# Gates of an RG-LRU group on 64-row halves put together by DMA, skipped zero products, time-step sums on four column groups, and down-weight sums moved to the FFN

## The chip, the cores and the metric

The kernel runs on one core of a Trainium2 chip. The metric is the device time of one execution in microseconds (us), the median over runs. A core has a matrix engine (TensorE), two engines for element-wise work (VectorE, ScalarE), GpSimd, and SyncE (SP), which here only issues DMAs; ScalarE issues DMAs too. Matrix results land in PSUM, everything else lives in SBUF (128 partitions) or in DRAM.

## The reference

One decoder layer on 2048 rows of 1024 numbers, all in float32. The normalised input goes through one projection. Its first 2048 columns feed an RG-LRU group, the rest a Mamba-2 SSD group; both outputs are normalised, joined, and projected back; a SwiGLU FFN of width 2816 follows. The parts that the change touches:

```
# RG-LRU: 16 blocks of 64 channels, each with its own 64x64 gate weights
r = sigmoid(einsum("btki,kij->btkj", xb, w_a) + b_a)
i = sigmoid(einsum("btki,kij->btkj", xb, w_x) + b_x)
log_a = -8 * r * softplus(-lam);  a = exp(log_a)
u = sqrt(-expm1(2 * log_a)) * (i * xf)
h_t = a_t * h_(t-1) + u_t

# SSD, in chunks of 128 time steps, 16 heads of 64, state of 128
a_cs = cumsum(dt * A) within a chunk
y_diag = (C B^T * exp(segsum(a))) x          # inside a chunk
states = carried from chunk to chunk (zero before the first)
y_off = exp(a_cs) * C * (state before the chunk)

# FFN
f = (silu(h @ w_gate) * (h @ w_up)) @ w_down
```

## The kernel before

**Precision.** A product of float32 quality is made of three matrix instructions on the type fp32r, high half times high, high times low, low times high (`mm3`, lines 135 to 137; `split`, lines 130 and 131, makes the halves: a cast on ScalarE, a subtraction on VectorE). Smaller products of plain float32 are listed as two instructions each.

**First stage (lines 260 to 720).** The 2048 time steps are two blocks (`b`) of 1024. Per block the kernel walks over the 37 column tiles of the input projection. Weights of a tile are loaded by SP (line 218) into one of the four `raw` buffers and split. For each tile, `col_product` issues 48 instructions of 128 columns by 512 into a `pp` buffer of PSUM (two of these). The mixes of a tile are Python generators (`ssd_mix`, `lru_mix`) whose pieces are woven into the column products of the next tile by `site` (`SITES` sets how many), so the small products stand between long runs of column products; a scheduler then settles the order on each engine. The small products use the two `pq` buffers of PSUM.

**The gates (`gates`, 363 to 379; `lru_mix`, 381 to 418).** For each of eight tiles of 128 channels, two 64-channel blocks stand side by side, so the weights of one gate are put as two 64x64 blocks on the diagonal of a 128x128 matrix, with zeros elsewhere. `lru_mix` splits the convolved input `lx` into `lh` and `ll` (lines 384, 385) and issues 12 instructions of 128 rows by 512: two gates, two halves of the time, three of `mm3`. ScalarE then runs two Tanh (393), Exp, Tanh, Square, and a square root (397 to 403), VectorE the rest up to the scan over time. Two different function tables are needed, so two table loads stand in it.

**The SSD group.** `ssd_dt3` (446 on) sums the time steps with a triangular matrix: eight products of 16 columns (line 456), one copy of 16x1024 (459), and one DMA to DRAM (`cs_dr`), which every mix reads back spread over partitions (520, 530). `ssd_mix` makes the states of the chunks (`pst`, 544; the carry `U`, 547), their part in the output (`po`, 551), and the part inside a chunk (`py`, 560), whose products are 64 columns wide and alternate between the two halves of the columns.

**Down-weight sums (`wdn_sums`, 569 to 580).** The FFN multiplies 2x2 blocks with seven products instead of eight, so sums of weight blocks are needed. For each of 11 `k`, four blocks of the down weights are loaded, combined by four subtractions (line 575 is the first) and stored to `t_dr`; table `WS` (line 31) puts these into the gate stage.

**FFN.** For each of 22 column tiles `fi` of a block, gate and up weights are loaded (740, 741) into two `raw` buffers, split and summed (744 on), and multiplied: seven products of 12 instructions each.

Of the kernel before, what the change touches and what calls it, by code (L numbers as in the profile page):

```python
# [15 lines left out]
P = 128  # L16
# [3 lines left out]
TB = 1024  # L20
# [10 lines left out]
WS = ((0, 2, 2, 0, 0, 0, 0, 0), (0, 2, 2, 1, 1, 1, 0, 0))  # L31
# [15 lines left out]
def hybrid_layer(ctx: ExitStack, tc: tile.TileContext, x, xT, w_in, w_dt, pack, heads, rows, wa, wx, w_out, w_gu, w_dn, out):  # L47
# [220 lines left out]
    with ExitStack() as fr:  # L268
# [95 lines left out]
        def gates(b, bd):  # L364
            st = wide("L").rearrange("p j (t k) l -> p (j t) k l", k=2)
            v.memset(st, 0.0)
            for j, ww in enumerate((wa, wx)):
                for h in range(2):
                    a.dma_start(out=st[64 * h:64 * h + 64, :, j, 64 * h:64 * h + 64],
                                in_=ww.rearrange("(t two) i j -> two i t j", two=2)[h])  # L370
            if b == 0:
                a.copy(out=bd, in_=st)
            res = []
            for q, z in enumerate(("Bt", "SM")):
                lo = tp.tile([P, 4, 2, P], F32R, name=z, bufs=1)
                qs = slice(4 * q, 4 * q + 4)
                v.tensor_sub(out=lo, in0=st[:, qs], in1=bd[:, qs].bitcast(F32))
                res.append(lo)
            return res

        def lru_mix(b, i, lx, gl, acc, bdl):
            th = []
# [12 lines left out]
            ci = c2[:, i:i + 1]  # L395
            av = t4()
# [4 lines left out]
            v.scalar_tensor_tensor(out=a2, in0=a2, scalar=1.0, in1=th[0], op0=ALU.add, op1=ALU.mult)  # L401
# [45 lines left out]
        def ssd_dt3(b, dt, dta):  # L447
# [7 lines left out]
            for c in range(NC):  # L455
                te.matmul(pr[0:NH, c * P:(c + 1) * P], lhsT=dta[:, c, :], rhs=tri, start=True, stop=True)
# [711 lines left out]
```

## Time and profile before

| | |
|---|---|
| median of 3 runs | 2625.59 us (2624.54 to 2626.57) |
| the profiled execution | 2623.91 us |
| its span, first to last instruction | 2622.1 us |
| TensorE busy | 2608.5 us, 99% of the span, 12357 matrix instructions |
| VectorE, ScalarE busy | 1849.3 us (71%), 1127.7 us (43%) |
| granted TensorE clock | 1.0 throughout |
| chain that ended last | TensorE 94%, VectorE 3%, ScalarE 1%, DMA 1% |

The profiled execution took 1.8 us more than its span and lies 1.7 us under the median. Matrix instructions are pipelined and overlap, so the time listed for one is longer than the step from its start to the next one's start; the price of one is read from starts.

### The profile page before, as it was taken

What the parts mean: (1) busy time and instruction counts of PE and PEld (TensorE: products, weight loads), DVE (VectorE), ACT (ScalarE), POOL (GpSimd) and SP (SyncE); (2) the same over time, 40 slices, a digit from 0 to 9 for tenths busy, and PEclk for the clock granted to TensorE, in tenths of its full rate; (3) what the DMA queues carried; (4) which work ended last, traced back from release to release, by engine and by line L of the source; (5) the groups of instructions that cost most, each with busy time, mean ns of one, the idle gap of its engine ahead of it and who ended that gap; (6) DMA issues with size and microseconds to landing.
All of it is one profiled execution on the core that took longest, in us unless ns stands there. A gap on an engine that the chain in (4) does not pass through costs nothing.

```text
span 2622.1 us, 31852 instructions
## 1 busy us (share of the span) xinstructions
PE 2608.5 (99%) x12357; PEld 2169.2 (83%) x12357; DVE 1849.3 (71%) x2698; ACT 1127.7 (43%) x1357; POOL 1.1 (0%) x8
## 2 busy tenths in 40 slices
PE   9999999999999999999999999999999999999998
PEld 8888888788888888888888888888888888888887
DVE  7997888878777867544478776778667774334676
ACT  7543466754544776333254332233222222322443
POOL 0000000000000000000000000000000000000000
PEclk9999999999999999999999999999999999999999
DMA  5332462224234526543464332235323234444664
GB/s 212 112 130 74 130 211 78 73 82 136 74 109 154 195 96 209 166 132 122 137 207 143 115 120 101 93 136 173 117 86 120 96 100 168 152 141 150 212 246 141
DMA packets 190279, 357.27 MB, mean 136 GB/s; under 512 B 18568, under 2 KB 91664, under 8 KB 190128
## 3 DMA queue, kind: packets, MB, share of 16 engines
q1 hardware_dynamic: 89504, 257.09, 30.4%
q10 hardware_dynamic: 100624, 98.15, 10.8%
q8 instruction: 97, 1.59, 0.2%
q14 instruction: 54, 0.44, 0.1%
HBM read 254.38 MB, written 100.80 MB: 135 GB/s over the span
## 4 chain that ended last, share of the span: by engine, by line
PE 94%; DVE 3%; ACT 1%; DMA 1%; issue 1%; SPq 0%; DVEq 0%; ACTq 0%
PE pf L136 16%; PE pf L135 16%; PE pf L137 16%; PE pp L135 11%; PE pp L137 11%; PE pp L136 11%; PE pq L136 3%; PE pq L137 3%; PE pq L135 3%; PE pq L560 1%; PE pq L539 1%; PE pq L551 1%; DMA L<-cs_dr 1%; DVE lx L309 1%; PE pq L523 1%
## 5 line engine op out<-in xcount | busy, mean ns | idle before, releaser
L135 PE MATMUL pp<-hx,s_hi 128*128 128x512 f32 x1392 | 547.2, 393 | 0.5 <-ACT s_hi L130 0.5
L137 PE MATMUL pp<-hx,s_lo 128*128 128x512 f32 x1392 | 543.8, 391 | 0.5 <-DVE s_lo L131 0.5
L136 PE MATMUL pp<-hx,s_hi 128*128 128x512 f32 x1392 | 543.1, 390 | 0.6 <-DVE hx L251 0.6
L130 ACT CAST s_hi<-raw 128x1024 fp32r<-128x1024 f32 (+1 forms) x167 | 170.3, 1022 | 373.6 <-PE pp L136 100.2
L135 PEld LDWEIGHTS pp<-hx,s_hi 128*128 128x128 f32 x1392 | 261.4, 188 | 56.1 <-issue 1.9
L137 PEld LDWEIGHTS pp<-hx,s_lo 128*128 128x128 f32 x1392 | 261.4, 188 | 55.5 <-DVE s_lo L131 0.8
L136 PEld LDWEIGHTS pp<-hx,s_hi 128*128 128x128 f32 x1392 | 261.5, 188 | 53.8 <-DVE hx L251 1.0
L135 PE MATMUL pf<-hx,s_hi 128*128 128x512 f32 x704 | 274.0, 389 | 0.0
L136 PE MATMUL pf<-hx,s_hi 128*128 128x512 f32 x704 | 273.9, 389 | 0.0
L137 PE MATMUL pf<-hx,s_lo 128*128 128x512 f32 x704 | 273.9, 389 | 0.0
L1008 DVE TENSOR_TENSOR d_lo<-draw,d_hi 128x1024 fp32r<-128x1024 f32 (+1 forms) x110 | 121.2, 1129 | 172.0 <-ACT d_hi L1007 171.8
L131 DVE TENSOR_TENSOR s_lo<-raw,s_hi 128x1024 fp32r<-128x1024 f32 (+1 forms) x167 | 197.9, 1187 | 61.4 <-ACT s_hi L130 57.1
L130 ACT CAST s_hi<-S 128x1024 fp32r<-128x1024 f32 x86 | 90.3, 1050 | 254.8 <-PE pf L136 239.1
L1007 ACT CAST d_hi<-draw 128x1024 fp32r<-128x1024 f32 (+1 forms) x110 | 104.7, 980 | 214.1 <-PE pf L136 181.1
L136 PE MATMUL pf<-d_lo,d_hi 128*128 128x512 f32 x504 | 196.1, 389 | 0.0
L137 PE MATMUL pf<-d_hi,d_lo 128*128 128x512 f32 x504 | 195.9, 389 | 0.0
L135 PE MATMUL pf<-d_hi 128*128 128x512 f32 x504 | 194.6, 389 | 0.0
L137 PEld LDWEIGHTS pf<-hx,s_lo 128*128 128x128 f32 x704 | 132.1, 188 | 27.4
L135 PEld LDWEIGHTS pf<-hx,s_hi 128*128 128x128 f32 x704 | 132.1, 188 | 27.4
L136 PEld LDWEIGHTS pf<-hx,s_hi 128*128 128x128 f32 x704 | 132.1, 188 | 27.4
L309 DVE SCALAR_TENSOR_TENSOR lx<-xr,pk,lx 128x1024 f32<-128x1024 f32 x108 | 138.2, 1280 | 10.2 <-ACT lx L306 9.1
L137 PE MATMUL pf<-hy,s_lo 128*128 128x512 f32 x356 | 138.5, 389 | 0.0
(342 smaller groups left out, 4512.8 us busy)
## 6 DMA issues: line engine op xcount, KB each, us to landing
raw<-w_gu_dram SPq DMA_DIRECT2D x86, 512.0 KB, 4.3
f_dr<-fo ACTq DMA_DIRECT2D x154, 256.0 KB, 4.5
raw<-w_in_dram SPq DMA_DIRECT2D x72, 512.0 KB, 3.4
draw<-f_dr SPq DMA_DIRECT2D x57, 512.0 KB, 4.4
L<-cs_dr SPq DMA_DIRECT2D x32, 512.0 KB, 5.5
g_dr<-t ACTq DMA_DIRECT2D x32, 512.0 KB, 3.3
raw<-g_dr SPq DMA_DIRECT2D x32, 512.0 KB, 4.9
raw<-h_dr SPq DMA_DIRECT2D x26, 512.0 KB, 4.2
```

The lines of the kernel that those rows point to most:

```text
L130: a.copy(out=hi, in_=raw)
L131: v.tensor_sub(out=lo, in0=raw, in1=hi.bitcast(F32))
L135: te.matmul(o, lhsT=wh, rhs=hi, start=start, stop=False)
L136: te.matmul(o, lhsT=wh, rhs=lo, start=False, stop=False)
L137: te.matmul(o, lhsT=wl, rhs=hi, start=False, stop=stop)
L309: v.scalar_tensor_tensor(out=y, in0=xr[:, k:k + TB], scalar=cw(k), in1=y, op0=ALU.mult, op1=ALU.add)
L523: te.transpose(pt[:, c].rearrange("p j d -> p (j d)"), xc[:, c * P:(c + 1) * P], ident)
L539: te.matmul(pst[:, c, :], lhsT=Bt[:, c, :], rhs=xe[:, c].rearrange("p j d -> p (j d)"), start=True, stop=True)
L551: te.matmul(po[:, c, :], lhsT=(sc[:, xi, :] if c == 0 else U[:, c - 1, :]), rhs=C[:, c * P:(c + 1) * P], start=True, stop=True)
L560: te.matmul(py[64 * j:64 * j + 64, c, :], lhsT=xd[:, c, j, :], rhs=L[:, j, c, :], start=True, stop=True)
L1007: a.copy(out=hi, in_=r)
L1008: v.tensor_sub(out=lo, in0=r, in1=hi.bitcast(F32))
```

## The change

- **Gates.** The weights of a tile are no longer put on a diagonal: rows 0 to 63 hold the blocks of r and i of the first 64 channels side by side, rows 64 to 127 those of the second 64 (i and r). Each of the 12 instructions of a mix now reads 64 rows, and its two halves `h` alternate between rows 0 to 63 and 64 to 127, into two `pq` buffers. The result of each half holds r and i of 64 channels on different partitions; after Tanh, four DMAs on SP of 64 partitions by 1024 (line 394 of the new kernel) put r together in one tile and i in another. The last mix of the last block does without them: four Tanh of 64 partitions each write to the right place.
- **Chain after the gates.** The Square and one Tanh of the full rate go; Tanh of half the rate takes its place, and (1 + a) is multiplied in later on VectorE, so its number of instructions there stays.
- **Weights of the gates** are arranged once, not once per block.
- **Skipped.** The product of the first chunk of the first block with a state that is zero (line 551, `c = 0`), and the last chunk's state of the last block, which nobody reads (line 544, with its two VectorE operations), for each of 8 mixes.
- **Time-step sums.** The eight products go to four groups of 32 columns; four copies of 16x256 on ScalarE and VectorE by turns and four DMAs take the place of one copy and one DMA.
- **Down-weight sums** go to the gate tiles 8 to 18 of the FFN's first block, and use two `raw` buffers each instead of two tiles of the first stage.

```diff
-        def gates(b, bd):
-            st = wide("L").rearrange("p j (t k) l -> p (j t) k l", k=2)
-            v.memset(st, 0.0)
...
+        def gates(hi, lo):
+            st = wide("L")[:, 0]
+            for h in range(2):
+                for j, ww in enumerate((wa, wx)):
+                    q = slice(64 * (h ^ j), 64 * (h ^ j) + 64)
+                    a.dma_start(out=st[64 * h:64 * h + 64, :, q],
                                 in_=ww.rearrange("(t two) i j -> two i t j", two=2)[h])
...
-            for j in range(2):
-                pr = pq.tile([P, TB], F32, name="pq")
-                for hh in range(2):
-                    s = slice(hh * HB, (hh + 1) * HB)
-                    mm3(pr[:, s], bd[:, i, j, :], bdl[i // 4][:, i % 4, j, :], lh[:, s], ll[:, s], True, True)
-                t = t4()
-                a.activation(out=t, in_=pr, func=AF.Tanh, scale=0.5, bias=hb[:, 8 * j + i:8 * j + i + 1])
-                th.append(t)
+            prs = [pq.tile([P, TB], F32, name="pq") for _ in range(2)]
+            for hh in range(2):
+                s = slice(hh * HB, (hh + 1) * HB)
+                for n, (w, z) in enumerate(((bd, lh), (bd, ll), (bdl, lh))):
+                    for h in range(2):
+                        q = slice(64 * h, 64 * h + 64)
+                        te.matmul(prs[h][:, s], lhsT=w[q, i, :], rhs=z[q, s], start=(n == 0), stop=(n == 2))
+            us, th = [t4(), t4()], [t4(), t4()]
+            for h, t in enumerate(us):
+                bias = hb[:, 8 * h + i:8 * h + i + 1]
+                if b + 1 < NB or i < 7:
+                    a.activation(out=t, in_=prs[h], func=AF.Tanh, scale=0.5, bias=bias)
+                for j in range(2):
+                    q = slice(64 * (h ^ j), 64 * (h ^ j) + 64)
+                    o = th[j][64 * h:64 * h + 64, :]
+                    if b + 1 < NB or i < 7:
+                        sy.dma_start(out=o, in_=t[q, :])
+                    else:
+                        a.activation(out=o, in_=prs[h][q, :], func=AF.Tanh, scale=0.5, bias=bias[q])
+            ci, cj = c2[:, i:i + 1], ch[:, i:i + 1]
+            t2, av = us
+            a.activation(out=t2, in_=th[0], func=AF.Tanh, scale=cj, bias=cj)
             a.activation(out=av, in_=th[0], func=AF.Exp, scale=ci, bias=ci)
-            a.activation(out=th[0], in_=th[0], func=AF.Tanh, scale=ci, bias=ci)
-            a2 = t4()
-            a.activation(out=a2, in_=av, func=AF.Square)
...
-            a.activation(out=a2, in_=a2, func=AF.Sqrt, scale=-0.25)
+            v.tensor_scalar(out=t2, in0=t2, scalar1=0.0, scalar2=None, op0=ALU.min)
+            a.activation(out=t2, in_=t2, func=AF.Sqrt, scale=-0.25)
             v.scalar_tensor_tensor(out=th[1], in0=th[1], scalar=1.0, in1=lx, op0=ALU.add, op1=ALU.mult)
-            v.tensor_mul(out=th[1], in0=th[1], in1=a2)
+            v.scalar_tensor_tensor(out=th[1], in0=av, scalar=1.0, in1=th[1], op0=ALU.add, op1=ALU.mult)
+            v.tensor_mul(out=th[1], in0=th[1], in1=t2)
...
             for c in range(NC):
-                te.matmul(pr[0:NH, c * P:(c + 1) * P], lhsT=dta[:, c, :], rhs=tri, start=True, stop=True)
-            cr = t4()[0:NH, :]
-            v.tensor_copy(out=cr, in_=pr[0:NH, :])
-            sy.dma_start(out=cs_dr[b], in_=cr)
+                o = slice(32 * (c % 4), 32 * (c % 4) + NH)
+                te.matmul(pr[o, c // 4 * P:(c // 4 + 1) * P], lhsT=dta[:, c, :], rhs=tri, start=True, stop=True)
+            for q in range(4):
+                o = slice(32 * q, 32 * q + NH)
+                (v.tensor_copy if q % 2 else a.copy)(out=cr[o, :], in_=pr[o, 0:2 * P])
+                sy.dma_start(out=cs_dr[b].rearrange("h (c q t) -> h c q t", q=4, t=P)[:, :, q, :],
+                             in_=cr[o, :].rearrange("h (c t) -> h c t", t=P))
...
-            for c in range(NC):
+            for c in range(NC if b + 1 < NB else NC - 1):
                 te.matmul(pst[:, c, :], lhsT=Bt[:, c, :], rhs=xe[:, c].rearrange("p j d -> p (j d)"), start=True, stop=True)
...
-            for c in range(NC):
+            c0 = 0 if b else 1
+            for c in range(c0, NC):
                 te.matmul(po[:, c, :], lhsT=(sc[:, xi, :] if c == 0 else U[:, c - 1, :]),
...
+        def wdn_sums(k):
+            r = [raw_tile() for _ in range(2)]
+            for q in range(2):
+                sy.dma_start(out=r[q].rearrange("p (q c) -> p q c", c=HB),
+                             in_=w_dn[2 * q:2 * q + 2, :, k, :].rearrange("q p c -> p q c"))
+            (b11, b12), (b21, b22) = ((z[:, :HB], z[:, HB:]) for z in r)
+            v.tensor_sub(out=b11, in0=b12, in1=b11)
+            v.tensor_sub(out=b12, in0=b22, in1=b12)
+            v.tensor_sub(out=b22, in0=b22, in1=b11)
+            v.tensor_sub(out=b21, in0=b21, in1=b22)
+            for o, z in enumerate((b11, b22, b12, b21)):
+                a.dma_start(out=t_dr[o][:, k, :], in_=z)
...
+                if b + 1 < NB and 0 <= fi - 8 < KF:
+                    wdn_sums(fi - 8)
```

The order on the engines, at three places. On TensorE, the fifth gate mix of the second block; `pp` is a column product, `pq` a gate product, `t4` the halves of the gate's input. Before:

```order
L137 MATMUL pp_6864<-hx_3882,s_lo_6695 128x512
L135 MATMUL pq_6919<-t4_6860,bd_2341 128x512
L136 MATMUL pq_6919<-t4_6861,bd_2341 128x512
L137 MATMUL pq_6919<-t4_6860,SM_6116 128x512
...
L135 MATMUL pq_6928<-t4_6860,bd_2341 128x512
L136 MATMUL pq_6928<-t4_6861,bd_2341 128x512
L137 MATMUL pq_6928<-t4_6860,SM_6116 128x512
```

and in the changed kernel (each line number is one lower above the gates):

```order
L136 MATMUL pp_6737<-hx_3852,s_lo_6579 128x512
L384 MATMUL pq_6792<-t4_6733,bd_2347 128x512
L384 MATMUL pq_6793<-t4_6733,bd_2347 128x512
L384 MATMUL pq_6792<-t4_6734,bd_2347 128x512
L384 MATMUL pq_6793<-t4_6734,bd_2347 128x512
L384 MATMUL pq_6792<-t4_6733,bdl_2348 128x512
L384 MATMUL pq_6793<-t4_6733,bdl_2348 128x512
```

The 12 instructions stay, at the same place; the two row halves now alternate, with nothing between them. Over the whole first stage 94 of the 96 pairs of halves stand next to each other, in 21 runs.

On ScalarE, the same mix; `t4` tiles are the gates, `xr` and `lx` the convolution of the next tile. Before:

```order
L305 COPY xr_6953<-pp_6864 128x1024
L393 ACTIVATE t4_6926<-pq_6919,hb_2342 128x1024
L306 ACTIVATE lx_6955<-pp_6864,pk_109 128x1024
L393 ACTIVATE t4_6935<-pq_6928,hb_2342 128x1024
L397 ACT_TABLE_LOAD
L397 ACTIVATE t4_6937<-t4_6926,c2_2344 128x1024
L398 ACTIVATE t4_6926<-t4_6926,c2_2344 128x1024
L400 ACTIVATE t4_6940<-t4_6937 128x1024
L403 ACT_TABLE_LOAD
L403 ACTIVATE t4_6940<-t4_6940 128x1024
```

and now:

```order
L304 COPY xr_6829<-pp_6737 128x1024
L305 ACTIVATE lx_6831<-pp_6737,pk_109 128x1024
L389 ACTIVATE t4_6806<-pq_6792,hb_2349 128x1024
L389 ACTIVATE t4_6807<-pq_6793,hb_2349 128x1024
L399 ACTIVATE t4_6806<-t4_6808,ch_2352 128x1024
L400 ACT_TABLE_LOAD
L400 ACTIVATE t4_6807<-t4_6808,c2_2351 128x1024
L402 ACT_TABLE_LOAD
L402 ACTIVATE t4_6806<-t4_6806 128x1024
```

Line 399 reads `t4_6808`, which the DMAs fill from both results of line 389; nothing stands between, so ScalarE waits there.

On SP, in the FFN stage where the down-weight sums now stand, the changed kernel has

```order
L866 DMA raw_11423<-w_dn_dram 128x2x512
L866 DMA raw_11424<-w_dn_dram 128x2x512
L734 DMA raw_11546<-w_gu_dram 128x1024
L735 DMA raw_11547<-w_gu_dram 128x1024
L866 DMA raw_11571<-w_dn_dram 128x2x512
```

where before pairs of gate and up weights (lines 740, 741) follow each other. A pair of down weights takes the `raw` buffers of the gate and up pair just split, and the next gate and up pair takes them after the sums are stored.

## Rows read from the trace of the kernel before

**Rows 1.** Page of the kernel before, parts 1, 2 and 4.
```profile
PE 2608.5 (99%) x12357; PEld 2169.2 (83%) x12357; DVE 1849.3 (71%) x2698; ACT 1127.7 (43%) x1357; POOL 1.1 (0%) x8
...
PEclk9999999999999999999999999999999999999999
...
PE 94%; DVE 3%; ACT 1%; DMA 1%; issue 1%; SPq 0%; DVEq 0%; ACTq 0%
```

**Rows 2.** Timeline of TensorE, 924 to 949 us: start, us, engine, line, tiles, shapes, count, idle before.
```profile
924.16 0.39 PE L135 MATMUL pq<-t,bd 128*128 128x512 f32 x1
...
926.92 0.40 PE L135 MATMUL pp<-hx,s_hi 128*128 128x512 f32 x1
...
948.74 0.39 PE L135 MATMUL pq<-t,bd 128*128 128x512 f32 x1
```

**Rows 3.** Timeline of TensorE around one mix of the SSD group, 124 to 129 us.
```profile
124.58 0.38 PE L551 MATMUL pq<-Cc,sc 128*128 128x128 f32 x2
124.80 1.73 PE L551 MATMUL pq<-Cc,t 128*128 128x128 f32 x14
126.46 1.97 PE L560 MATMUL pq<-L,t 128*64 128x128 f32 x32
128.35 0.50 PE L135 MATMUL pp<-hx,s_hi 128*128 128x512 f32 x1
128.69 0.40 PE L136 MATMUL pp<-hx,s_hi 128*128 128x512 f32 x1
```

**Rows 4.** Timeline of ScalarE, 928 to 937 us, in one gate stage.
```profile
928.08 1.13 ACT L393 ACTIVATE t<-pq,hb 128x1024 f32<-128x1024 f32 x1
929.23 1.28 ACT L397 ACT_TABLE_LOAD   x1
930.52 1.24 ACT L397 ACTIVATE t<-t,c 128x1024 f32<-128x1024 f32 x1
931.80 1.24 ACT L398 ACTIVATE t<-t,c 128x1024 f32<-128x1024 f32 x1
...
936.01 1.06 ACT L403 ACTIVATE t<-t 128x1024 f32<-128x1024 f32 x1 [0.72 <-DVE t L402]
```

**Rows 5.** Timeline of VectorE in the same stage: the low half for the next gates.
```profile
941.95 1.22 DVE L385 TENSOR_TENSOR t<-lx,t 128x1024 fp32r<-128x1024 f32 x1
```

**Rows 6.** Tile bd, 820 to 1000 us: the weight load of a gate product, ns min/median/max.
```profile
L135 PEld LDWEIGHTS pq<-t,bd x32: 187/188/192, 825.6 to 998.3; 128*128 128x128 f32 x32
```

**Rows 7.** Timeline of TensorE at the time-step sums of the second block.
```profile
559.62 1.92 PE L456 MATMUL pq<-tri,dtx 128*16 128x128 f32 x16
```

**Rows 8.** DMA issues of the whole run: tiles, queue, count, KB each, median us to landing.
```profile
raw<-w_gu_dram SPq DMA_DIRECT2D x86, 512.0 KB, 4.3
...
L<-w_dn_dram SPq DMA_DIRECT2D x44, 256.0 KB, 4.9
t_dr<-L ACTq DMA_DIRECT2D x44, 256.0 KB, 3.2
...
out_dram<-fx ACTq DMA_DIRECT2D x16, 256.0 KB, 2.2
```

**Rows 9.** Line 530, the loads t<-cs_dr of 256 KB: all 32, to landing.
```profile
DMA to landing us min/median/max: 4.5/6.7/9.9
```

**Rows 10.** Waits of the DMA queue SP: who for whom, us in total, times, longest.
```profile
SPq L218 <- DVE s_lo L131: 433.3, 48, 25.9
```

**Rows 11.** Timeline of TensorE at 463 us: its wait for the low half of a gate input.
```profile
463.40 0.50 PE L136 MATMUL pq<-t,bd 128*128 128x512 f32 x1 [0.73 <-DVE t L385]
```

**Rows 12.** Groups of instructions by line: busy, mean ns, idle before. One sum of down weights.
```profile
L575 DVE TENSOR_TENSOR L<-L 128x512 f32<-128x512 f32 x11 | 7.6, 689 | 6.5 <-DMA L<-w_dn_dram 4.2 <-DMA t_dr<-L 1.1 <-issue 1.0
```

**Rows 13.** Timeline of VectorE in the FFN stage: first and last read of one raw pair.
```profile
1582.32 0.69 DVE L744 TENSOR_TENSOR S<-raw 128x512 f32<-128x512 f32 x1
...
1587.13 1.22 DVE L131 TENSOR_TENSOR s_lo<-raw,s_hi 128x1024 fp32r<-128x1024 f32 x1
```

**Rows 14.** Timeline of ScalarE in the FFN stage: casts of the next period.
```profile
1598.73 1.05 ACT L130 CAST s_hi<-S 128x1024 fp32r<-128x1024 f32 x1 [4.40 <-PE pf L136]
```

More of the change, by code (lines that the diff above doesn't have):

```diff
@@ L362, in lru_proj, with lru_mix @@
             return lx, gate_of(pg, AF.Gelu_apprx_tanh, b == 0)
-        def gates(b, bd):
-            st = wide("L").rearrange("p j (t k) l -> p (j t) k l", k=2)
-            v.memset(st, 0.0)
-            for j, ww in enumerate((wa, wx)):
-                for h in range(2):
-                    a.dma_start(out=st[64 * h:64 * h + 64, :, j, 64 * h:64 * h + 64],
-                                in_=ww.rearrange("(t two) i j -> two i t j", two=2)[h])
[L371 to L382, printed above, removed]
+        def gates(hi, lo):
[4 more added lines that the diff above has]
+                    a.dma_start(out=st[64 * h:64 * h + 64, :, q],
+                                in_=ww.rearrange("(t two) i j -> two i t j", two=2)[h])
+            a.copy(out=hi, in_=st)
+            v.tensor_sub(out=lo, in0=st, in1=hi.bitcast(F32))
+        def lru_mix(b, i, lx, gl, acc):
             lh, ll = (tl.tile([P, TB], F32R, name="t4", bufs=NT4) for _ in range(2))
@@ L537, in ssd_mix @@
             pst = pq.tile([P, NC, P], F32, name="pq")
-            for c in range(NC):
+            for c in range(NC if b + 1 < NB else NC - 1):
                 te.matmul(pst[:, c, :], lhsT=Bt[:, c, :], rhs=xe[:, c].rearrange("p j d -> p (j d)"), start=True, stop=True)
             U = t4((P, NC, P))
-            for c in range(NC):
+            for c in range(NC if b + 1 < NB else NC - 1):
                 for j in range(2):
@@ L549, in ssd_mix @@
             po = pq.tile([P, NC, P], F32, name="pq")
-            for c in range(NC):
+            c0 = 0 if b else 1
+            for c in range(c0, NC):
                 te.matmul(po[:, c, :], lhsT=(sc[:, xi, :] if c == 0 else U[:, c - 1, :]),
@@ L647, in hybrid_layer @@
         v.tensor_scalar(out=amat, in0=amat, scalar1=-1.0, scalar2=None, op0=ALU.mult)
-        wk = 0
         for b in range(NB):
@@ L668, in hybrid_layer @@
             if b == 0:
-                bd = fc.tile([P, 8, 2, P], F32R, name="bd")
+                bd, bdl = (fc.tile([P, 8, P], F32R, name=z) for z in ("bd", "bdl"))
                 hb = fc.tile([P, 16], F32, name="hb")
@@ L672, in hybrid_layer @@
                 c2 = fc.tile([P, 8], F32, name="c2")
+                ch = fc.tile([P, 8], F32, name="ch")
                 nl = fc.tile([P, 8], F32, name="nl")
@@ L676, in hybrid_layer @@
                 v.tensor_scalar(out=c2, in0=c2, scalar1=-4.0, scalar2=None, op0=ALU.mult)
+                v.tensor_scalar(out=ch, in0=c2, scalar1=0.5, scalar2=None, op0=ALU.mult)
             nhT = {}
@@ L708, in hybrid_layer @@
                 if i == 0:
-                    bdl = gates(b, bd)
+                    if b == 0:
+                        gates(bd, bdl)
                     sumsq(b, 1, acc)
                     acc = tl.tile([P, TB], F32, name="acc", bufs=1)
-                for _ in range(WS[b][i]):
-                    wdn_sums(wk)
-                    wk += 1
-                stages.append(lru_mix(b, i, *xs, acc, bdl))
+                stages.append(lru_mix(b, i, *xs, acc))
             hT = nhT
```

29 lines of the change are left out of this document (9 added, 20 removed).

## The prediction

> **What bounds the kernel now.** I read the page first [rows 1]: TensorE is busy 99% of the span, 94% of the chain that ended last is TensorE, and every slice of the granted clock shows a 9, so the clock stands at its upper level (2.4 GHz) throughout. So only two things can move the time: TensorE work that goes or comes, and new waits of TensorE. The other engines count only through such waits.
>
> The busy time can't price an instruction, since the listed 0.39 us of a 128x512 one overlaps its neighbours. Starts can. The timeline of TensorE in a gate stage [rows 2]: gates begin at 924.16, the next column product at 926.92, so 12 gate instructions take 2.76 us, **0.230** each. In the SSD group [rows 3], two plain float32 instructions of 128 columns, one product, take 124.80 - 124.58 = **0.22** us.
>
> The third view is what the gates feed. ScalarE's second Tanh ends at 929.21 and its square root starts at 936.01, 6.80 us later [rows 4]; VectorE ends the low half for the next gates at 941.95 + 1.22 = 943.17 [rows 5]; the next gates start at 948.74 [rows 2]. So one step lasts 24.58 us and this chain has 5.57 us to spare.
>
> **Gates.** Sixteen mixes of 12 instructions stay, but two instructions of 64 rows each, on different rows and into different buffers, can run side by side. That it works is shown only for columns: in line 560, 32 instructions alternate between two halves of the columns and take 128.35 - 126.46 = 1.89 us [rows 3], 0.118 for a pair with its share of the switch, whereas plain ones take (126.46 - 124.80) / 14 = 0.119 each. So there a pair costs what one costs, and I take the same for rows: 94 adjacent pairs save 0.230 each, **-21.6 us**. The bounds are none (0) and all.
>
> Switching to halves and back costs something. Two plain instructions take 0.22, rounded, so about 0.1125 each. Then the 14 before line 560 take 1.66 instead of 1.57 (+0.09), its 32 in pairs 1.89 instead of 1.80 (+0.09), and the first full one after them 128.69 - 128.35 = 0.34 instead of 0.23 (+0.11) [rows 3]. That is 0.29; I take 0.30 for each of 21 runs, **+6.3**. Row halves can lie above this or below: 0 if the array needn't empty, and 0.6, twice as much, if 64-row instructions must be over before full ones start. That gives 0 to +12.6. The Trainium skill (TensorEngine Tiling (Array Packing), Key Properties) says that changing the tiling mode, not only the tile, drains TensorE; it speaks against short runs like these, the rows agree by the 0.29 us, and without it the sum would end 6.3 us lower.
>
> **Weight loads.** Every matrix instruction has one load [rows 1]. A gate's load lasts 187 to 192 ns [rows 6]; two in a row would be 0.376 us, more than the 0.230 of the pair. Against that, the 14 instructions of 128 columns have a load each and follow at 0.119 [rows 3], so two take 0.237 at most, about the pair's own time. I keep the pair at 0.230, and 0.376 as a rival. The Trainium skill (TensorE: Matmul & The Clock Gate, LDWEIGHTS) says that a load's time goes by its columns and not by its rows, P/1.2 ns; by that, halving the rows leaves each load as long as before, an estimated 0.107 us and 0.213 for two, and the sum stays. The row's 0.188 is longer than that figure.
>
> **Skipped products.** Eight of line 551 and eight of line 544, at 0.22 each: **-3.5**. The VectorE operations that go are off the chain.
>
> **Time-step sums.** Sixteen instructions with 1.92 us busy [rows 7], two blocks. On four column groups they would need between a quarter (0.45) and a half (0.9) of 16 x 0.112 = 1.79, and a switch of 0.3: from +0.3 (nothing side by side) to -1.0 per block. I take -0.85, near the lower end, since line 560 shows pairs at full gain: **-1.7**. The four copies and four DMAs take the place of one each; the mix that reads them comes a full column product later, some 11 us (48 x 0.230), against a landing of 2.2 to 9.9 [rows 8, 9]; without that cover, a few us once per block.
>
> **The wait for the DMAs.** After: second Tanh, DMA d, Tanh 1.24, table load 1.28, Exp 1.24, table load 1.28, square root [durations in rows 4]: d + 5.04 instead of 6.80, a change of d - 1.76. The Square that went and the 0.72 idle [rows 4] pay for part of the wait. No transfer within SBUF is in the trace. The nearest of 256 KB are a store of VectorE's sums, 3.2, and a store of results, 2.2 [rows 8]; above it, reads spread over partitions with 4.5 / 6.7 / 9.9 [rows 9]. I take d = 3.2, since a swap reads SBUF in plain rows as that store does: the chain gets 1.44 longer. TensorE's step gets shorter by 6 x 0.230 - 0.30 = 1.08. Of the 5.57 to spare, 3.05 are left, so the wait costs nothing until **d = 6.25**.
>
> Behind the waiting Tanh, ScalarE's order has casts of later weights; on SP, loads that wait for `raw` buffers stand ahead of the swaps. SP waits for line 131 often, 433.3 us in 48 waits, up to 25.9 [rows 10]. I count nothing for this: the splits which free these buffers stand in VectorE's order ahead of the convolution of this mix, so are over before the second Tanh. If that is wrong, it acts as a longer d.
>
> In the first block the chain is tighter: TensorE already waits 0.73 for a low half at 463.40 [rows 11]. The new order puts 24 column products (5.5 us) there between the first gates and the rest, which may take that wait away (-0.7); or one or two mixes run 1.44 late. I take one, **+1.4**, bounds -0.7 to +2.9.
>
> **Down-weight sums.** In the gate stage 11 x 4 subtractions of 0.689 us go from VectorE [rows 12], which is no gain for TensorE. In the FFN, a `raw` pair is free when line 131 ends at 1587.13 + 1.22 = 1588.35 [rows 13]. Then load 4.9 [rows 8], four subtractions 2.8 [rows 12], stores that ScalarE issues behind a cast at 1598.73, 10.4 later [rows 14], landing 3.2, load of gate and up weights 4.3 [rows 8]: about 10.4 + 1.05 + 1.1 (a second cast) + 3.2 + 4.3 = 20, with queueing some 23. The weights are wanted after two tiles, 2 x 84 x 0.229 = 38.5, less the 6 us for splitting (1588.35 - 1582.32): 32. Some 9 us to spare: nothing.
>
> **Sum.** -21.6 + 6.3 - 3.5 - 1.7 + 1.4 = **-19.1**. The profiled execution of 2623.9 becomes 2604.8; it lies 1.7 under the median, so the median becomes **2606.5**. With the good ends (switches 0, sums -2.0, waits -0.7) it is 2598; with the bad ends (+12.6, +0.6, +2.9) 2617. I take 2597 to 2617 as the forecast's own range.
>
> **Rivals.**
> *Halves one after the other.* If two 64-row instructions don't run side by side, the gates give nothing and the switches stay: 6.3 - 3.5 - 1.7 + 1.4 = +2.5, so 2628; without the switches 2622. For it: no row product is in the trace, so the change may not do what it means to. Against it: line 560 [rows 3]. Chance 0.09.
> *Loads bound the pair.* At 0.376 for a pair only 94 x (0.460 - 0.376) = 7.9 is saved: 2606.5 + 13.7 = 2620. For it: [rows 6]. Against it: the pace of 0.119 with a load each. 0.06.
> *Slower: the swap's wait decides.* If the four DMAs, issued one after another on SP beside the weight loads, land later than 6.25 us after the second Tanh, the gates of the next mix wait for VectorE's low half, once per mix. In 14 mixes the gain is eaten from d = 6.25 + 19.1 / 14 = 7.6; at the longest landing, 9.9 [rows 9], the time is 2606.5 + 14 x 3.65 = 2658. For it: the median of 6.7 among reads of this size; against it: those are spread over partitions from DRAM, and stores of 256 KB take 2.2 to 3.2 [rows 8]. 0.06.
> *Buffers in the FFN.* If the down-weight chain takes over 32 us, each second tile is late; at 4 us late in five of them, 2627. Against it: 9 us to spare. 0.04.
>
> **How the numbers follow.** The forecast has 0.75; a measurement of this kernel can tell 0.2%, 5.2 us, from no change, so faster begins below 2620.3. The forecast lies there, and half of the loads' rival: faster 0.78. Same: halves in turn 0.09, buffers 0.04, the other half of the loads' 0.03: 0.16. Slower: the swap's wait, 0.06. The range takes the forecast's own with a little for other small waits and reaches to the loads' rival: 2596 to 2621, leaving out about 0.2.
>
> **What would show it.** The gates of one mix should last about 1.4 to 1.7 us from first start to the next column product, not 2.76, with starts of a pair almost together. At 2.8 and more, halves run in turn; at about 2.3, loads bind. ScalarE should idle some 3 us before the Tanh of line 399, released by the swap DMA, and TensorE should not wait for line 376's low half by more than a few us in all; idle of TensorE there of over 1 us per mix means that the swap decides. In the FFN no split should wait for a load of gate and up weights. The forecast is wrong if the gate stage's step doesn't shrink by about 1.1 us per mix.

## The result, and the profile after the change

The changed kernel takes 2639.62 us (median of 4 runs, 2637.87 to 2645.23), the one before beside it 2626.08 (4 runs, 2624.54 to 2628.14). The ratio is 1.0054 with a 95% interval of 1.0042 to 1.0066: slower by half a per cent, where 2606.5 was forecast. Its profiled execution took 2639.88 us with a span of 2638.1.

The page of the changed kernel, parts 1, 2 and 4:

```profile
PE 2600.5 (99%) x12325; PEld 2148.3 (81%) x12325; DVE 1839.1 (70%) x2688; ACT 1109.4 (42%) x1343; POOL 1.1 (0%) x8
...
PEclk9999999999999999999999999999999999999999
...
PE 85%; DVE 5%; ACT 4%; DMA 4%; issue 1%; SPq 0%; ACTq 0%; DVEq 0%
```

Against [rows 1], TensorE's share of the chain fell from 94% to 85%. The busy shares and the clock in slices of 66 us show next to nothing; the waits must be looked for one by one. First the part that came as forecast: TensorE's timeline in the first gate stage of the second block.

```profile
834.52 0.73 PE L384 MATMUL pq<-t,bd 64*128 64x512 f32 x4
835.08 0.40 PE L384 MATMUL pq<-t,bdl 64*128 64x512 f32 x2
835.32 0.63 PE L384 MATMUL pq<-t,bd 64*128 64x512 f32 x4
835.78 0.39 PE L384 MATMUL pq<-t,bdl 64*128 64x512 f32 x2
836.10 0.50 PE L134 MATMUL pp<-hx,s_hi 128*128 128x512 f32 x1
836.44 0.39 PE L135 MATMUL pp<-hx,s_hi 128*128 128x512 f32 x1
```

Twelve 64-row products take 836.10 - 834.52 = 1.58 us, against 2.76 [rows 2]: a pair costs what one full product costs. The first full product after them takes 0.34 instead of 0.23, as it did after column groups [rows 3].

Where the time went is read from the start of the same column product in both timelines (they are in the same order in both kernels):

| place | before, us | after, us | after less before |
|---|---|---|---|
| third mix of the first block done | 403.1 | 398.2 | -4.9 |
| end of the first block's gates | 502.5 | 498.1 | -4.3 |
| beginning of the second block | 528.9 | 533.6 | +4.7 |
| its first SSD mix | 582.5 | 585.4 | +2.9 |
| its second SSD mix | 611.1 | 621.2 | +10.1 |
| its fourth gate mix | 909.6 | 914.2 | +4.6 |
| its last gate mix | 1009.4 | 1021.8 | +12.4 |
| output projection | 1065.7 | 1082.6 | +16.8 |

So the gain is there wherever TensorE runs on, and is lost at a few places: about 9 us from 498 to 534 us, 7 at 593 us, and 12 from 914 to 1083 us. The last five gate mixes of the first block together gain nothing net (-4.9 to -4.3), since TensorE waits 2.85, 0.65 and 0.81 us for a low half at 411, 434 and 464 us. In the FFN nothing is lost, and about 1 us comes back where a wait goes. The waits of TensorE in the changed kernel (engine, line, for whom: us in total, times, longest) name the places:

```profile
PE pq L384 <- DVE t L376: 6.2, 5, 2.9
PE pp L188 <- DVE hx L178: 5.3, 4, 2.5
PE pq L527 <- DVE t L561: 4.8, 1, 4.8
PE pp L134 <- ACT hx L249: 2.7, 1, 2.7
```

L376 is the low half of a gate's input, L178 the next block's input, L561 the first SSD mix of the second block, L249 the scaled output weights at the end of the block. At three places the granted clock falls to 0.50 after TensorE has waited: from 501.6 to 511.8, from 597.2 to 604.0 and from 1003.3 to 1010.2 us. By windows, at the first block's end (us, then busy time and count of TensorE, its weight loads, VectorE, ScalarE, GpSimd, then the granted clock, the share of the DMA engines and GB/s):

```profile
494.00:502.00 8.00, 5.49 (x23) 4.01 (x23) 8.00 (x10) 7.17 (x10) 0.00 (x0) 0.97 0.17 61
502.00:510.00 8.00, 5.22 (x10) 2.33 (x11) 8.00 (x9) 3.79 (x4) 0.00 (x0) 0.50 0.21 66
```

TensorE idles some 2.5 us of the first stretch, and in the next the granted clock is 0.50, its lower level of 1.2 GHz; VectorE is busy throughout.

The swap: the DMAs of line 394, to landing, and what ScalarE waited for before line 399.

```profile
DMA to landing us min/median/max: 3.1/4.9/8.7
```

```profile
  DMA t<-t: 69.1, 12
```

In 12 mixes ScalarE waited 69.1 us, 5.8 each, for the swap. From the end of the second Tanh to the start of line 399, the prediction's d, it is 3.5 to 8.2 us over the fifteen mixes with a swap, 5.8 in the mean, and over 6.25 in five; I had taken 3.2. A d is more than one landing: SP issues the four DMAs one after another, they land about 1.2 us apart, and line 399 needs the third. The chain that ended last, around the time-step sums (start, us, what):

```profile
567.70 2.75 DMA cs_dr<-t
570.96 9.38 DMA L<-cs_dr
580.43 2.30 DVE L L537
...
585.12 2.68 DVE t L548 x14
587.80 2.20 DVE L L551
...
598.28 1.94 PE pq L527 x8
```

The store of the last of four pieces, then the spread read, 9.38 us, stand on the path; VectorE's queue behind it ends late, and the transposes at 598.28 are what TensorE waited for.

### The profile page after: what moved, and what is told of

Same layout as the page of the kernel before. It is cut to its first block, busy times and chain, and to the rows that moved or that the text cites. A ratio compares the mean times of both kernels' runs of the same rounds, so it can differ in the third digit from the quotient of the medians.

```text
span 2638.1 us, 31886 instructions
## 1 busy us (share of the span) xinstructions
PE 2600.5 (99%) x12325; PEld 2148.3 (81%) x12325; DVE 1839.1 (70%) x2688; ACT 1109.4 (42%) x1343; POOL 1.1 (0%) x8
## 4 chain that ended last, share of the span: by engine, by line
PE 85%; DVE 5%; ACT 4%; DMA 4%; issue 1%; SPq 0%; ACTq 0%; DVEq 0%
PE pf L135 16%; PE pf L134 16%; PE pf L136 16%; PE pp L134 9%; PE pp L135 9%; PE pp L136 9%; PE pq L134 2%; PE pq L135 2%; PE pq L136 2%; DMA t<-t 2%; PE pq L568 1%; PE pq L556 1%; PE pq L543 1%; DVE t L406 1%; DMA L<-cs_dr 1%
```

## The experiments

All are compared with the kernel before on the same chip, by medians.

**1. Time-step sums as before, in the changed kernel.**

```diff
-                te.matmul(pr[o, c // 4 * P:(c // 4 + 1) * P], lhsT=dta[:, c, :], rhs=tri, start=True, stop=True)
-            for q in range(4):
...
+                te.matmul(pr[0:NH, c * P:(c + 1) * P], lhsT=dta[:, c, :], rhs=tri, start=True, stop=True)
+            cr = t4()[0:NH, :]
+            v.tensor_copy(out=cr, in_=pr[0:NH, :])
+            sy.dma_start(out=cs_dr[b], in_=cr)
```

> The changed kernel with the time-step sums as before (one partition group, one copy of 16x1024, one DMA); all else as changed. Theory A, two DMA chains each came onto the path (the four small DMAs of the time-step sums in the second block, and the swap DMAs of the gates): the 4.8 us wait and the 4 us at the low clock at 593 to 604 us go, 7 to 8 us, and the 1.7 us that four column groups save come back, so about 2634, 5 to 6 us under the changed kernel. Rival B, that wait only collects what TensorE gained earlier and the time-step sums have no part in it: no gain, about 2641.

Measured 2632.25 us, ratio 1.0029 (1.0016 to 1.0042): 7.4 under the changed kernel. The step from the first to the second SSD mix, +7.2 us in the table, is +0.3 here. With the four small DMAs gone the wait is gone; theory A held, B fell. Experiment 4 shows that part of the 7.4 hangs on how early TensorE comes there.

**2. No swap DMAs: four Tanh of 64 partitions in every mix.**

```diff
-                if b + 1 < NB or i < 7:
+                if False:
                     a.activation(out=t, in_=prs[h], func=AF.Tanh, scale=0.5, bias=bias)
...
-                    if b + 1 < NB or i < 7:
+                    if False:
                         sy.dma_start(out=o, in_=t[q, :])
```

> The changed kernel without swap DMAs: in every mix four Tanh of 64 partitions write r and i to their places, as the last mix does already. Four cost 2 x 1.1 us more of ScalarE than two, so the chain from the former second Tanh to the square root becomes 7.2 us, against 6.8 before the change and 10 to 13 with the swap. Theory A: the waits at 408, 498 to 511 and 970 to 1046 us go, about 27 us, so 2613. Rival C, 64-row products lower the granted clock, or TensorE simply arrives too early at places where VectorE is the bound: 2630 to 2640, with the low clock still there at 501 to 511 us.

Measured 2634.30, ratio 1.0035 (1.0022 to 1.0047): 5 us under the changed kernel, not 27. Theory A fell: without any swap the waits at the block's end stay. The time lies in rival C's range, and the low clock that it named is there too:

```profile
507.00:515.00 8.00, 5.70 (x12) 3.42 (x13) 8.00 (x10) 3.90 (x4) 0.00 (x0) 0.50 0.28 87
```

Of rival C's two reasons, experiments 7 and 9 rule out the first: there 64-row products run at a granted clock of 1.0.

**3. Both edits,** with the two diffs above.

> Both of these edits together. Theory A: row halves, skips and moved down-weight sums keep their gain without either DMA chain, 2606 to 2610, faster than both kernels; granted clock 1.0. Rivals B and C: not under 2630.

Measured 2630.48, ratio 1.0020 (1.0011 to 1.0030), just inside "not under 2630": theory A (2606 to 2610) fell, rivals B and C held, and the time stays 24 us above the forecast's 2606.5 without either DMA chain. In the list of TensorE's waits stand

```profile
PE pp L188 <- DVE hx L178: 4.4, 4, 1.7
PE pq L384 <- DVE t L376: 4.3, 2, 4.2
PE pp L134 <- ACT lx L305: 2.3, 1, 2.3
PE pq L135 <- DVE wob L250: 2.0, 3, 1.2
```

These are the waits of the gates' input and of the two block ends again, with neither DMA chain left. By the same column products, every mix gains 1.0 us up to 452 us (-7.9 there); then 4.1 are lost at 455 us, 8.9 from 498 to 533, and 8.7 from 980 to 1071.

**4. Old gates, all else changed.**

```diff
-        def gates(hi, lo):
+        def gates(b, bd):
...
-            prs = [pq.tile([P, TB], F32, name="pq") for _ in range(2)]
+            for j in range(2):
+                pr = pq.tile([P, TB], F32, name="pq")
...
+                    mm3(pr[:, s], bd[:, i, j, :], bdl[i // 4][:, i % 4, j, :], lh[:, s], ll[:, s], True, True)
```

> The changed kernel with the gates as before (full diagonal weights, 12 products of 128 rows, no swap DMAs, old chain); skips, time-step sums on four groups and moved down-weight sums stay. Theory A: 2626 - 3.5 - 1.7 + 8 for the wait at the time-step sums = 2629. Rival B (that wait only collects earlier gains): 2621.

Measured 2623.17, ratio 0.9990 (0.9981 to 1.0000), nearer to rival B's 2621 than to theory A's 2629. Hardly a wait at the block ends; the wait at the time-step sums is there, but 2.6 us instead of 4.8:

```profile
PE pq L526 <- DVE t L560: 2.6, 1, 2.6
```

From the first to the second SSD mix 4.0 us are lost here, against 7.2 in the changed kernel, so the four DMAs cost less where TensorE comes later. The block-end losses come with the row halves and whatever puts r and i together: without them the kernel is not slower than before.

**5. Full gates with the new, shorter chain and old time-step sums.** Skips and moved sums are left of the change; the weights of the gates are arranged in each block again.

```diff
                 for j in range(2):
...
+                    for hh in range(2):
+                        s = slice(hh * HB, (hh + 1) * HB)
+                        mm3(prs[j][:, s], bd[:, i, j, :], bdl[i // 4][:, i % 4, j, :], lh[:, s], ll[:, s], True, True)
+                    a.activation(out=th[j], in_=prs[j], func=AF.Tanh, scale=0.5, bias=hb[:, 8 * j + i:8 * j + i + 1])
```

> The changed kernel with full diagonal gates (12 products of 128 rows, r and i written in place by two Tanh, no swap DMAs), the new chain without Square, and the time-step sums as before. Left of the change: skipped products, moved down-weight sums, shorter ScalarE chain. Theory A (both DMA chains and the row halves made the loss): 2.9 us under before as in the run with old gates, less the 4.0 us wait at 586 us, plus 2 x 1.2 that the four column groups saved: about 2621, faster than before. Rival D (moving the down-weight sums or the skips costs something too): 2625 or more.

Measured 2621.93, ratio 0.9988 (0.9978 to 0.9997): theory A held, and these parts gain about what they should.

**6 and 7. Row halves with four Tanh in the second block alone: all eight mixes, or (with `NHALF = (0, 5)`) the first five.** In these and the following kernels a number for each block says in how many of its first mixes halves are used:

```diff
+NHALF = (0, 8)
...
+            if i < NHALF[b]:
...
+                        a.activation(out=th[j][o, :], in_=prs[h][q, :], func=AF.Tanh, scale=0.5, bias=hb[o, 8 * j + i:8 * j + i + 1])
+            else:
```

> The same, but row halves with four Tanh of 64 partitions in all eight mixes of the second block; the first block keeps full gates. Theory E, row halves pay only until TensorE runs into a place where VectorE or ScalarE sets the pace, and there the idle time and the low clock after it take more than the gain: eight steps of -1.0 in the second block, no loss at 455 and 499 to 512 us (12.9 us in the run with halves everywhere), but the 8.7 us at the end of the second block stay: 2621 - 8 + 8.7 = 2622. Rival F, the loss at the end only collects a delay from the first block: 2613.

> The same with row halves only in the first five mixes of the second block. Theory E: five steps of -1.0; TensorE then has three normal steps before the end of the block, so part of the loss there goes: 2616 to 2621. Rival F: 2616.

Measured 2622.06, ratio 0.9988 (0.9978 to 0.9997), and 2617.15, ratio 0.9966 (0.9954 to 0.9978). Both steps as theory E had them: each mix gains 1.0 us, and with halves in the last three mixes too, 10.2 us are lost after them, from 983 to 1066 us. There the eight-mix kernel waits

```profile
PE pp L135 <- ACT lx L306: 2.2, 1, 2.2
PE pq L136 <- DVE wob L251: 2.0, 3, 1.2
PE pq L408 <- ACT t L396: 1.3, 1, 1.3
```

**8. Down-weight sums back in the gate stage,** on top of the third experiment.

```diff
-                if b + 1 < NB and 0 <= fi - 8 < KF:
-                    wdn_sums(fi - 8)
...
+                for _ in range(WS[b][i]):
+                    wdn_sums(wk)
+                    wk += 1
```

> The run with four Tanh everywhere and old time-step sums (2630.5), with the down-weight sums back in the gate stage: 44 more subtractions of 0.69 us on VectorE there, four or eight of them in mixes 1 and 2 of each block. Theory E (VectorE sets the pace in the first block and at its end): 3 to 10 us slower, 2633 to 2640, with longer waits before 512 us. Rival G (VectorE has room, only ScalarE's order counts): 2630 again.

Measured 2635.48, ratio 1.0040 (1.0025 to 1.0055): 5.0 us slower than the third. Much of that is not where theory E looked for it. By column products some 3 us go in the first stage and as much in the FFN, where the first product of the down projection now waits for `f`, which is read back from DRAM and split,

```profile
PE pf L135 <- ACT d_hi L1015: 3.3, 1, 3.3
```

so the range was met for another reason in good part. Moving the sums was a gain of 5.0 us here, and not the nothing that the prediction put.

**9. Halves in the first three mixes of the first block, and five of the second.**

```diff
-NHALF = (0, 5)
+NHALF = (3, 5)
```

> The run with row halves in the first five mixes of the second block (2617.2), and in the first three mixes of the first block too. Theory E: three steps of -1.0 bring TensorE 3 us earlier to 499 to 512 us, where VectorE builds the next block's inputs; it waits there and the gain is lost, or more than that if the clock falls: 2617 to 2621. Rival H (only the late mixes of the first block, with four Tanh each, make that loss): 2614.

Measured **2613.81** (4 runs, 2613.35 to 2614.01), ratio 0.9957 (0.9942 to 0.9972), the lowest median here (the intervals of experiments 14 to 16 overlap with its own) and faster than both kernels. Rival H came true and theory E fell: TensorE comes to the end of the first block 6.1 us earlier than before, and hardly waits. The windows of experiment 9:

```profile
494.00:502.00 8.00, 7.28 (x32) 5.36 (x31) 8.00 (x10) 5.76 (x8) 0.00 (x0) 1.00 0.21 67
502.00:510.00 8.00, 8.00 (x37) 6.57 (x36) 6.43 (x9) 3.02 (x3) 0.00 (x0) 1.00 0.54 199
```

VectorE is just as full in the first stretch, so a full VectorE alone is not the cause; what loses lies in the last mixes of the block. The granted clock stays at 1.0 although eight mixes run on 64-row products.

**10. Twenty filling products at the block's end,** on top of the third experiment.

```diff
+        if wl is None and hh == 1 and len(ks) == KD and not ks[0]:
+            for _ in range(20):
+                te.matmul(o, lhsT=wh[:, 0:P], rhs=hT[KD - 1, 0][1], start=True, stop=True)
```

> The run with four Tanh everywhere and old time-step sums (2630.5), with 20 products of 128x512 whose result is overwritten, put ahead of the first product that waits for the next block's inputs (about 500 us). They add 20 x 0.227 = 4.5 us of TensorE work where it idles 4.4 us. Theory I, the low clock at 502 to 512 us follows from that idle time and costs some 4 us beyond it: the clock stays at 1.0 there and the time falls to 2626. Rival J (VectorE alone sets the pace there, the clock costs nothing): 2630 or a little more.

Measured 2628.81, ratio 1.0013 (1.0004 to 1.0022), against 1.0020 (1.0011 to 1.0030) without: the intervals overlap. The windows of experiment 10:

```profile
494.00:502.00 8.00, 8.00 (x37) 6.64 (x36) 6.85 (x7) 7.41 (x9) 0.00 (x0) 1.00 0.00 0
502.00:510.00 8.00, 6.13 (x26) 4.24 (x24) 8.00 (x10) 3.83 (x6) 0.00 (x0) 1.00 0.20 66
```

The clock stays up, so its fall follows from the idle time. But of the 35.3 us that the stretch between the same two column products takes in the third experiment (26.4 before) it takes back only some 2.2 (33.0, filling included); these lengths are from one profiled execution each, so 2 us is an estimate. The time lies between theory I's 2626 and rival J's 2630. Theory I had the mechanism and about twice its size: most of the loss is waiting.

**11. Eight of VectorE's subtractions on GpSimd,** on top of the third experiment.

```diff
-                v.tensor_sub(out=lo, in0=z, in1=hi.bitcast(F32))
+                (g if hh else v).tensor_sub(out=lo, in0=z, in1=hi.bitcast(F32))
```

> The run with four Tanh everywhere and old time-step sums (2630.5), with the low halves of the second part of the next block's inputs (8 subtractions of 0.68 us at 495 to 511 us) on GpSimd instead of VectorE. Theory E (VectorE is the bound there): its queue is 5.4 us shorter, TensorE waits less, 2624 to 2627. Rival L (another engine's order is the bound, or GpSimd is too slow): 2630 or more.

Measured 2629.27, ratio 1.0017 (1.0007 to 1.0026), no clear difference: a subtraction takes 1.3 to 3.3 us there instead of 0.68, and TensorE waits for GpSimd instead.

```profile
PE pp L188 <- POOL hx L178: 5.0, 4, 1.5
```

Inconclusive on VectorE, since the replacement was slow.

**12. The swap DMAs instead of four Tanh, in the five mixes of experiment 7.**

```diff
-                        a.activation(out=th[j][o, :], in_=prs[h][q, :], func=AF.Tanh, scale=0.5, bias=hb[o, 8 * j + i:8 * j + i + 1])
+                    a.activation(out=us[h], in_=prs[h], func=AF.Tanh, scale=0.5, bias=hs[:, 8 * h + i:8 * h + i + 1])
...
+                        sy.dma_start(out=th[j][o, :], in_=us[h][q, :])
```

> The run with row halves in the first five mixes of the second block (2617.2), with two Tanh of 128 partitions and the four swap DMAs of the change in these five mixes instead of four Tanh. Theory A, the DMAs take 6 to 8 us and make the chain of a mix longer than TensorE's step of 23.6 us: as in the changed kernel the steps of the later mixes stop gaining, 1 us each in two or three of them: 2619 to 2621. Rival K (there is room for them in the second block): 2617.

Measured 2625.91, ratio 1.0001 (0.9992 to 1.0011): 8.8 us slower than experiment 7, more than twice the upper expectation. The profiled execution, 2629.52, is the slowest of ten. The DMAs land after 3.1/4.7/5.6 us there, and the chain that ended last goes through them:

```profile
883.20 5.59 DMA t<-t
890.15 1.28 ACT L317
...
898.58 1.23 DVE t L397
899.85 2.50 PE pq L408 x10
```

From the swap over ScalarE to the low half (L397) for which TensorE waits. But the scheduler's order on ScalarE changed with the edit. In each of the five mixes an activation of line 317 with its table load now stands between the Tanh behind the swap and the Exp, in ScalarE's timeline

```profile
888.89 1.24 ACT L423 ACTIVATE t<-t,ch 128x1024 f32<-128x1024 f32 x1 [1.93 <-DMA t<-t]
890.15 1.28 ACT L317 ACT_TABLE_LOAD   x1
891.45 1.03 ACT L317 ACTIVATE t<-pp 128x1024 f32<-128x1024 f32 x1
892.49 1.28 ACT L424 ACT_TABLE_LOAD   x1
```

where experiment 7 has

```profile
855.18 1.25 ACT L422 ACTIVATE t<-t,ch 128x1024 f32<-128x1024 f32 x1
856.44 1.28 ACT L423 ACT_TABLE_LOAD   x1
```

From that Tanh to the square root it is 7.46 us, against 5.11 in experiment 7. So the 8.8 us, as much as the halves gain, are the price of the swap and of this order together; how much is due to each is not shown.

**13. Two dead Tanh in the last five mixes of the first block of experiment 9,** which have full gates.

```diff
+                    if b == 0:
+                        a.activation(out=us[j], in_=prs[j], func=AF.Tanh, scale=0.5, bias=hb[:, 8 * j + i:8 * j + i + 1])
```

> The run with row halves in the first three mixes of the first block and the first five of the second (2613.8), with two more Tanh of 128 partitions, whose results nobody reads, in the last five mixes of the first block, which keep their full gates: their chain gets the 2.2 us longer that four Tanh cost, TensorE's work stays. Theory M, a longer chain of ScalarE and VectorE in these mixes, which also normalise and split the next block's inputs, is what loses there: waits at 455 and 499 to 512 us come back, 8 to 12 us, 2622 to 2626. Rival N (row halves or TensorE's early arrival lose there): 2614.

Measured 2622.52, ratio 0.9987 (0.9978 to 0.9997): 8.7 us slower, with no row half added. TensorE's waits and the window with them:

```profile
PE pp L189 <- DVE hx L179: 4.7, 4, 2.2
```

```profile
502.00:510.00 8.00, 5.23 (x12) 3.39 (x13) 8.00 (x9) 4.46 (x6) 0.00 (x0) 0.61 0.22 78
```

The stretch that took 26.9 us in experiment 9 takes 33.7. Theory M holds for the block's end: 2.2 us of ScalarE more per mix, with the order that the scheduler made of them, bring back the wait there and the low clock, though TensorE's work is the same. The wait at 455 us that it also named did not come back.

**14 to 16. How far halves may go, and the column groups with one DMA.** `NHALF` is (4, 6) in 14 and 15, (3, 6) in 16; in 15 and 16 the four copies go into one tile of 16 partitions:

```diff
+            cr = t4()[0:NH, :]
...
+                (v.tensor_copy if q % 2 else a.copy)(out=cr.rearrange("h (c q t) -> h c q t", q=4, t=P)[:, :, q, :],
+                                                     in_=pr[o, 0:2 * P].rearrange("h (c t) -> h c t", t=P))
+            sy.dma_start(out=cs_dr[b], in_=cr)
```

> Row halves with four Tanh in the first four mixes of the first block and the first six of the second, else as the 2613.8 run. Theory M: the chains of these two further mixes still have room: two steps of -1.0, 2612. If the room is used up there: 2614 to 2617.

> The same with the time-step sums on four column groups, put together by four copies into one tile of 16 partitions and stored by one DMA. Theory A (the four DMAs made the wait at 593 us): TensorE saves 2 x 1.2 us and does not wait: 2610. Rival O (four copies are late enough by themselves): a wait of about 1 to 3 us at 590 us, 2612 to 2614.

> Row halves with four Tanh in the first three mixes of the first block and the first six of the second; time-step sums on four column groups with one DMA; skips and moved down-weight sums as in the change. Against the 2613.8 run: one more step of -1.0 and 2 x 1.2 us for the column groups: 2610 to 2612. Rival O (the four copies bring a wait back): 2613 or more.

Measured 2615.77 (ratio 0.9962, 0.9947 to 0.9977), 2616.13 (0.9963, 0.9949 to 0.9977; runs from 2611.7 to 2619.2) and 2614.77 (0.9956, 0.9942 to 0.9970). The first lies in the range for "room used up", the second in neither of its two ranges, the third in rival O's. The fourth mix of the first block brings a wait of 2.3 us at 455 us: its room is used up, while the sixth of the second block still gains 1.0. With one DMA the second block keeps what the column groups save (-1.5 instead of -0.3 us between 556 and 582 us, no wait after); but in the last run the first block waits for the sums once,

```profile
PE pq L591 <- issue: 3.4, 1, 3.4
```

from 99 to 102 us, where VectorE and ScalarE have to build L from what was read back. Against experiment 9 nothing is gained in all.

## Why the prediction was wrong

**Gates: right.** Forecast was that a pair of halves costs what one product costs and a run of them 0.30 us more, 1.08 us per mix; measured are 1.0 us per mix, wherever no wait comes between. Halves in turn and loads that bind, the two rivals on TensorE, fell with the 1.58 us. The rule of the Trainium skill (TensorEngine Tiling (Array Packing), Key Properties) that a changed tiling mode drains TensorE agrees with the trace: 1.58 - 6 x 0.23 = 0.20 within a run and 0.34 - 0.23 = 0.11 after it, 0.31 in all.

**Skips right, moved sums worth more than nothing.** Each SSD mix starts 0.25 us earlier (0.22 forecast; the state product that goes is the one of line 539 of the kernel before, and line 544 is its VectorE operation). No split in the FFN waits for a load, as forecast. But the move was put at nothing, and experiment 8 shows 5.0 us for it, there in a kernel with four Tanh.

**Time-step sums: the saving right, the cover wrong.** The first column product after the sums, before and then after the change:

```profile
561.47 0.50 PE L135 MATMUL pp<-hx,s_hi 128*128 128x512 f32 x1
```

```profile
564.55 0.50 PE L134 MATMUL pp<-hx,s_hi 128*128 128x512 f32 x1
```

The sums take 0.56 us (from 563.99 to 564.55) where they took 561.47 - 559.62 = 1.85 [rows 7], so 1.29 per block are saved where 0.85 was taken. The step that failed: "the mix that reads them comes a full column product later, some 11 us". The four stores follow one another (565.7 to 567.7, the last landing 2.75 later) and the reads, issued together, take 9.4; TensorE waits 4.8 us for the chain of the mix behind them, and a low clock after that wait adds to it. 7.4 us lost in all (experiment 1). I had named that cover and priced its loss at "a few us", without putting it into the sum.

**The wait for the DMAs: the price was wrong, and the room was read at one place.** This is the step that turns the sign, and it has two halves. The price: "I take d = 3.2"; measured are 5.8 in the mean and 8.2 at most. I took the lower of two neighbours for a transfer of which none was in the trace, and counted one transfer where four are issued in turn.

The room: "3.05 are left", so no cost until 6.25, was read from one mix, the fifth of the second block, and used for nearly all sixteen; for the tight mixes of the first block I took 1.44 once. In the gate mixes of the second block it held. Two rows of ScalarE with d = 7.49, then TensorE's wait:

```profile
908.08 2.12 ACT L389 ACTIVATE t<-pq,hb 128x1024 f32<-128x1024 f32 x2
917.68 1.24 ACT L399 ACTIVATE t<-t,ch 128x1024 f32<-128x1024 f32 x1 [7.49 <-DMA t<-t]
930.02 0.50 PE L384 MATMUL pq<-t,bd 64*128 64x512 f32 x2 [0.71 <-DVE t L376]
```

and one with d = 6.12, behind which TensorE does not wait:

```profile
869.17 1.24 ACT L399 ACTIVATE t<-t,ch 128x1024 f32<-128x1024 f32 x1 [6.12 <-DMA t<-t]
```

In the late mixes of the first block it did not hold: there TensorE waits 0.65 us behind a d of 3.85. At the two block ends it did not hold either. The late mixes of the first block also normalise and split the next block's inputs on VectorE and ScalarE, and the last ones of the second block scale the output weights. Experiment 13 shows that 2.2 us more of ScalarE in each of five mixes at the end of the first block cost 8.7 us, and experiments 7 and 9 that in eight other mixes four Tanh in place of two leave the 1.0 us of each mix whole. With four Tanh everywhere and the old time-step sums the time still stays 24 us above the forecast (experiment 3). So the room at the block ends is the larger failure, and the price of the swap comes on top.

So the rival "the swap's wait decides" came true in part: slower, by ScalarE's wait and VectorE's low half. Its form, the same loss in each of 14 mixes from a d of 7.6 on, did not: for the low half TensorE waits 6.2 us in all, far from the 1 us per mix that was to be its sign. Most of the loss sits at the block ends and behind the time-step sums, and four Tanh, which take ScalarE 2.2 us longer, lose at the block ends too (experiment 3). Judged by the tightest mixes, a time above the kernel before should have had far more than 0.06.

**The clock: not in the forecast at all.** In the changed kernel TensorE's waits near 500, 594 and 1000 us are followed by stretches of 7 to 10 us at a granted clock of 0.50, its lower level. Experiment 10 puts the price at an estimated 2 us for one such place; waiting is the larger part.

What stays open: how the 8.8 us of experiment 12 are shared between the swap and ScalarE's changed order; why the four time-step DMAs cost 7.2 us behind the row halves and 4.0 without them; and what makes the waits near 455 us, which experiment 13 did not bring back. In experiment 13 the scheduler's order on ScalarE and VectorE moved somewhat too, so the 2.2 us and that order are not told apart. Experiment 11 did not settle whether VectorE or the order on it holds the block's end.

## What to carry to other kernels

Read the room of a chain at its tightest place, not at a typical one: a step of TensorE that gets shorter while its chain on the other engines gets longer pays in the stages with room, and can lose more than it gains where the other engines have extra work, since TensorE then waits there and a low clock can follow the wait. Applied only to mixes with room, with four Tanh in place of the swap and the time-step sums as before, the same halves gave 2613.8 us. A transfer of a kind that the trace does not hold, put into a chain, should be priced by the slow neighbour until it is measured, and with all that are issued in a row ahead of the one that is needed.

## What the runs showed of the hardware

Two products of 64 rows on the two halves of the rows, into different buffers, take as long as one of 128 rows, apart from 0.2 us per run (12 in 1.58 us against 2.76); eight products on four groups of 32 columns take 0.56 us where they took 1.85 in one (559.62 in [rows 7] to 561.47). DMAs of 256 KB within SBUF took 3.1 to 8.7 us to land beside other loads. Four Tanh of 64 partitions took 4.52 us in experiment 7, two of 128 took 2.12 in the changed kernel. A subtraction of 128x512 on GpSimd took 1.3 to 3.3 us, on VectorE 0.68. In the changed kernel the granted clock stood at 0.50 of full for 7 to 10 us after TensorE had idled for a few; with filling products in the idle time it stayed at 1.0 (experiment 10).
